# A GLA and short-convolution decoder step on one core: the sample's states through column groups of the array, and another order around the last head's norm

## The chip, the core and the metric

The kernel runs on one NeuronCore of a Trainium2 chip. Its engines work side by side and wait for each other through semaphores: TensorE (PE, matrix products; its weight loads are listed as PEld), VectorE (DVE), ScalarE (ACT), GpSimd (POOL), and SyncE (SP), which here only issues DMAs. The metric is the device time of one execution in microseconds, the median of several runs. The profile is one further execution taken by the hardware profiler; its span is the time from its first to its last instruction.

## What is computed

One inference step of a two-layer decoder, width 1024. The tokens are one new sequence of 1024 tokens (the prompt) and 8 running sequences with 4 new tokens each (the sample). Layer 0 mixes with gated linear attention (GLA, 4 heads, key width 128, value width 256), layer 1 with a gated short convolution; each is followed by an MLP of width 4096, and each of the four parts ends with a LayerNorm of the scaled residual:

```python
x = layer_norm(ALPHA * x + h, ln1_g[i], ln1_b[i])                       # h: the mixer
x = layer_norm(ALPHA * x + mlp(x, mlp_w_up[i], mlp_w_down[i]), ln2_g[i], ln2_b[i])
```

In the GLA, a head's output is a part within the chunk of tokens and a part from the recurrent state, `o_inter = q_dec S_prev`, with a state of 128 x 256. The prompt starts from a zero state. Each of the 8 sample sequences brings its own state per head, so its four query columns meet a matrix that no other sequence uses. Everything is f32, and all outputs include the new states.

## The kernel before

Activations are kept transposed, channels on the 128 partitions and tokens along the free axis: Z holds 8 chunks of channels by 1056 tokens. In the GLA stage the tokens are worked on in three groups (`TGS`): 384, 384 and 288 columns, the last with 256 prompt tokens and the 32 of the sample. Big products split each f32 operand into a high and a low part in fp32r and run three passes (`mm3`, L234); small ones use plain f32 products (`mm`, L230), of which the profile lists two records each.

**A head.** `queries_keys` projects the queries and keys of the three groups, `core` (L588) walks the nine token tiles (eight of the prompt, the ninth the sample), `gated` (L572) projects the output gate of a group, applies SiLU (ScalarE) and multiplies (VectorE), then splits into `hh` and `hl`; `accumulate` (through `out(tg)`) multiplies by the output weights and adds into Z. For the ninth tile `core` calls `sample` (L667): `outputs` forms the 32 output columns from the values and the masked scores (`sTs`) and from the states: for each of the 8 sequences and each half of the value width one product of 128x128 state weights with 4 query columns. `products` and `state` then update the states through four row groups of the array, 32 rows each. In the profile, `raw` in these products is the buffer that holds the states.

**Delayed steps.** Work that belongs beside other work is put into chains by `after(key, (delay, step), ...)`. A counter, `clock`, advances by an estimate of PE's time with each product (`cost`); `tick()`, called after each projection or block of products, runs each chain's next step if its delay has passed; `need(key)` runs all that is left of a chain at once. This sets the order in which instructions are written. In this part of the kernel each engine's final order is set by the tile framework, which may place later work earlier where an engine would stand idle; in the MLP part the DMA queues of SP and POOL keep the written order.

**The last head and its LayerNorm.** The mean is already taken out: the output weights are centred, and Z is centred during the heads. `accumulate` squares each chunk (ScalarE), adds the squares (VectorE and POOL), and `layer_norm` (L315) runs four steps: `split` (sum and split of the squares), `var` (two products with ones), `rstd` (L289 to L297: logarithm, exponential and a Newton step), and `finish` for each of four pairs of chunks (one multiplication of two chunks on VectorE, L334, then scale and bias of each chunk on ScalarE, L336). The order in the last head is `gated` for all three groups, then `out(0)`, `out(1)`, `out(2)`, then `need` for the three norms.

**The MLP.** Products use a Strassen-like scheme with seven products over quarters; the first two, 1 and 2, read only the first 528 token columns, product 5 the others too. A product of the up-projection has 8 steps of 24 matmuls of 2 x 264 columns. Before it, its four blocks of activations are split into `bh` (ScalarE, L847) and `bl` (VectorE, L848), in a ring of five buffers; the weights likewise into `wh` and `wl`. A `big` buffer holds the differences for product 5.

Of the kernel before, what the change touches and what calls it, by code (L numbers as in the profile page):

```python
# [57 lines left out]
def hybrid_step(ctx, tc, x_prompt, x_sample, state_gla, state_conv, gla_w_in, gla_w_gate_up, gla_b_gate,  # L58
# [33 lines left out]
    ident = const.tile([P, P], F32, name="ident")  # L92
    make_identity(nc, ident)
# [56 lines left out]
    for g in (2, 3):  # L150
        V.tensor_add(seq, seq, seq1[:, g, :])

# [163 lines left out]
    def layer_norm(tg, sums, pg, pb):  # L316
# [3 lines left out]
        box = {}  # L320

# [10 lines left out]
        def finish(k):  # L332
            pair = z[:, k:k + 2, :]
            V.tensor_tensor(pair, pair, box["rstd"][:, :n].unsqueeze(1).to_broadcast([P, 2, n]), op=ALU.mult)  # L334
# [126 lines left out]
    with tc.tile_pool(name="gp", bufs=3) as gp:  # L461
# [110 lines left out]
        def gated(tg, m, ur, o, tags=("g", "g")):  # L572
# [9 lines left out]
            hh = gt(tags[0], [P, 384], 9 if tags[0] == "g" else 3, F32R)  # L582
            A.copy(hh[:, :n], sr[:, :n])
            hl = gt(tags[1], [P, 384], 9 if tags[1] == "g" else 3, F32R)
# [3 lines left out]
        def core(h, qkk, uv, dec, o):  # L588
# [77 lines left out]
            def sample(k2t, st, vt):  # L666
# [33 lines left out]
                after(("sample",), (0, outputs))  # L700
# [31 lines left out]
        for h in range(H):  # L732
# [34 lines left out]
            for tg in range(3):  # L767
                tags = [("g", "g")] * 2
# [22 lines left out]
    for tg in range(3):  # L791
# [21 lines left out]
    cbuf = work.tile([P, KC * 34], F32, name="cbuf")  # L813
# [54 lines left out]
    class Unit:  # L868
# [33 lines left out]
        def split(self):  # L902
# [3 lines left out]
            return self.parts  # L906

# [20 lines left out]
    def up(x, pairs, relu):  # L928
# [62 lines left out]
        for prod in UP:  # L991
            for i, (s, quad) in enumerate(pairs):
# [386 lines left out]

    mlp(0, Z, Z2)  # L1380
# [55 lines left out]
```

## Time and profile before

| | us |
|---|---|
| median of 3 runs | 2261.52 |
| lowest and highest run | 2258.97, 2264.5 |
| profiled execution, its own time | 2263.59 |
| span of the profiled execution | 2261.9 |
| mean granted TensorE clock, share of full | 0.983 |
| busy: PE, DVE, ACT, POOL | 2202.5, 1619.5, 1127.8, 524.7 |
| GLA stage, from the start to PE's last GLA product | about 513 |

A line of the profile names the line of the kernel, the engine, the operation, the tiles it writes and reads, and shapes. The page counts a matmul as busy until its modelled end, so consecutive ones overlap; the distance from start to start is what a product costs in a stream. Idle time before an instruction stands in brackets with what ended it. `ps` and `pq` are accumulators in PSUM, `g`, `ring` and `raw` buffers in SBUF.

### The profile page before, as it was taken

Reading aid. Unit: us, or ns where it says so; the run is one execution under the profiler, and the core shown is the slowest. Engines: PE = TensorE matmul, PEld = TensorE weight load, DVE = VectorE, ACT = ScalarE, POOL = GpSimd, SP = SyncE. Lnnn points to the kernel's source line nnn. Section 1 sums busy time; section 2 is a strip of 40 time slices with the busy share of each in tenths; the row PEclk is TensorE's granted clock in tenths of the full one; section 3 lists DMA queues with packets and bytes.
Section 4 is the critical chain, followed back from the end, with each engine's and each line's share of the span. In section 5 each row is a group of like instructions: output and inputs, shape, how many; then the busy total and the mean of one; then the engine's idle time right before and its main releaser. Section 6 shows DMA issues by size and latency. Waiting matters only on the chain. (4 is left out here: it accounts for less than half of the span.)

```text
span 2261.9 us, 43193 instructions
## 1 busy us (share of the span) xinstructions
PE 2202.5 (97%) x17341; PEld 2180.1 (96%) x17341; DVE 1619.5 (72%) x2982; ACT 1127.8 (50%) x2023; POOL 524.7 (23%) x551
## 2 busy tenths in 40 slices
PE   9999999996999999999999999998999999999996
PEld 8999999996999999999999999997999999999996
DVE  7474848467578864678787897996668875578877
ACT  4443525258563445564457444445855444654443
POOL 5202321221422021412021323220331101422121
PEclk9999999998999999999999999998999999999998
DMA  5120212113868456769353857760786734877546
GB/s 156 32 75 31 75 40 67 38 59 81 109 119 214 119 108 122 97 126 217 99 112 68 131 111 100 164 156 24 126 136 141 177 90 95 129 131 185 152 88 148
DMA packets 297476, 251.51 MB, mean 111 GB/s; under 512 B 15444, under 2 KB 238776, under 8 KB 297276
## 3 DMA queue, kind: packets, MB, share of 16 engines
q0 software_dynamic: 123200, 107.58, 31.2%
q1 hardware_dynamic: 174076, 141.18, 21.1%
q8 instruction: 136, 2.23, 0.4%
q14 instruction: 64, 0.52, 0.1%
HBM read 227.00 MB, written 9.12 MB: 104 GB/s over the span
## 5 line engine op out<-in xcount | busy, mean ns | idle before, releaser
L865 PE MATMUL pq<-bh,wh 128*128 128x264 f32 x4160 | 847.6, 285 | 9.3 <-ACT bh L847 7.3
L865 PE MATMUL pq<-bl,wh 128*128 128x264 f32 x4160 | 847.7, 285 | 5.0 <-DVE bl L848 5.0
L865 PE MATMUL pq<-bh,wl 128*128 128x264 f32 x4160 | 845.0, 285 | 1.8 <-DVE wl L848 1.7
L865 PEld LDWEIGHTS pq<-bh,wh 128*128 128x128 f32 x4160 | 646.2, 189 | 11.5 <-ACT bh L847 9.9
L865 PEld LDWEIGHTS pq<-bl,wh 128*128 128x128 f32 x4160 | 646.3, 189 | 6.1 <-DVE bl L848 5.8
L865 PEld LDWEIGHTS pq<-bh,wl 128*128 128x128 f32 x4160 | 646.2, 189 | 2.6 <-DVE wl L848 2.5
L847 ACT CAST wh<-raw 128x512 fp32r<-128x512 f32 x312 | 193.5, 621 | 398.2 <-PE pq L865 383.7
L848 DVE TENSOR_TENSOR wl<-raw,wh 128x512 fp32r<-128x512 f32 x312 | 214.4, 688 | 142.2 <-ACT wh L847 135.2
L854 POOL DMA_DIRECT2D SB<-in_mlp_w_up x128 | 163.5, 1329 | 430.8 <-DVE wl L848 223.8
L847 ACT CAST wh<-SB 128x512 fp32r<-128x512 f32 x208 | 128.7, 619 | 239.2 <-PE pq L865 213.4
L848 DVE TENSOR_TENSOR wl<-SB,wh 128x512 fp32r<-128x512 f32 x208 | 142.7, 686 | 85.3 <-ACT wh L847 85.3
L847 ACT CAST bh<-H 128x528 fp32r<-128x528 f32 (+1 forms) x292 | 165.3, 570 | 56.7 <-PE pq L865 51.3
L848 DVE TENSOR_TENSOR bl<-H,bh 128x528 fp32r<-128x528 f32 (+1 forms) x292 | 179.0, 625 | 15.4 <-ACT bh L847 15.2
L854 POOL DMA_DIRECT2D SB<-in_mlp_w_down x96 | 85.1, 1172 | 300.3 <-DVE wl L848 136.6
L236 PE MATMUL ps<-XH,whi 128*128 128x384 f32 (+1 forms) x384 | 128.6, 335 | 0.0
L237 PE MATMUL ps<-XL,whi 128*128 128x384 f32 (+1 forms) x384 | 127.5, 332 | 0.0
L238 PE MATMUL ps<-XH,wlo 128*128 128x384 f32 (+1 forms) x384 | 127.0, 331 | 0.0
L854 POOL DMA_DIRECT2D SB<-in_conv_w_in x48 | 61.2, 1295 | 168.8 <-DVE wl L848 60.4
L865 PE MATMUL pq<-bh,rh 128*128 128x264 f32 x320 | 94.0, 294 | 4.0 <-ACT bh L847 4.0
L865 PE MATMUL pq<-bl,rh 128*128 128x264 f32 x320 | 91.9, 287 | 0.2
L865 PE MATMUL pq<-bh,rl 128*128 128x264 f32 x320 | 91.5, 286 | 0.0
L963 ACT ACTIVATE H<-H 128x528 f32<-128x528 f32 x96 | 61.9, 645 | 46.9 <-DVE H L983 28.0
(275 smaller groups left out, 3620.4 us busy)
## 6 DMA issues: line engine op xcount, KB each, us to landing
raw<-in_mlp_w_down SPq DMA_DIRECT2D x160, 256.0 KB, 3.2
SB<-in_mlp_w_up POOLq DMA_DIRECT2D x128, 256.0 KB, 4.9
raw<-in_mlp_w_up SPq DMA_DIRECT2D x96, 256.0 KB, 2.9
SB<-in_mlp_w_down POOLq DMA_DIRECT2D x96, 256.0 KB, 7.8
SB<-in_mlp_w_up SPq DMA_DIRECT2D x64, 256.0 KB, 4.3
raw<-in_gla_w_in SPq DMA_DIRECT2D x24, 512.0 KB, 3.8
SB<-in_conv_w_in POOLq DMA_DIRECT2D x48, 256.0 KB, 4.8
raw<-SB POOLq DMA_DIRECT2D x36, 256.0 KB, 4.2
```

The costliest lines, as they stand in the source:

```text
L236: PE.matmul(out, wh, xh, start=first, stop=False)
L237: PE.matmul(out, wh, xl, start=False, stop=False)
L238: PE.matmul(out, wl, xh, start=False, stop=last)
L847: A.copy(hi[:, :w], src)
L848: V.tensor_sub(lo[:, :w], src, f32(hi[:, :w]))
L854: queue.dma_start(dst, src, **kw)
L865: PE.matmul(out[:, c:c + NT], w, b[:, n * NT:(n + 1) * NT], start=first and i == 0, stop=last and i == 2)
L963: A.activation(h, h, AF.Relu, scale=sign)
```

## The change

Four things are done.

- `sample`: a new step, `inter`, multiplies the 32 query columns (as 128x32 weights) with the states. For each half of the sequences four products of 256 columns go to four 32-partition strips of one PSUM bank, that is, to four column groups of the array. Each strip then holds all 32 query columns against one sequence's state; two VectorE operations pick the valid rows with the mask `seq` and add the halves into `x`. `outputs`, at least 2000 ns of PE's estimated time later, adds `x` to the output through one product per half of the value width with `rep4`, a matrix that folds the four strips back into 32 columns. The sixteen 4-column products go.
- The last head runs `out(0)` and `out(1)` before `gated` of the third group; the buffers' tags that the old order called for go.
- In `layer_norm`, the third group only stores the summed squares in `cbuf`, which is made at the start; the rest becomes `last_tokens`, a chain in the MLP with a delay of 3000 before each step. Its result is needed at product 5.
- In `layer_norm`, the second group's delays shrink, and every second chunk's scale and bias moves to VectorE.

```diff
+    rep4 = gconst.tile([P, NS], F32, name="rep4")
+    V.tensor_add(rep4, ident[:, 0:NS], ident[:, NS:2 * NS])
+    for g in (2, 3):
+        V.tensor_add(rep4, rep4, ident[:, g * NS:(g + 1) * NS])
...
+        if tg == 2:
+            V.tensor_add(cbuf, sums[0][:, :n], sums[1][:, :n])
+            return
...
-                A.activation(z[:, i, :], z[:, i, :], AF.Identity, scale=par[:, pg + i:pg + i + 1],
-                             bias=par[:, pb + i:pb + i + 1])
-        after(("x", tg), (1500, split), (D_VAR - 1500, var), (D_RSTD, rstd), *[(D_FIN, lambda k=k: finish(k)) for k in range(0, KC, 2)])
+                g, b = par[:, pg + i:pg + i + 1], par[:, pb + i:pb + i + 1]
+                if i == k:
+                    A.activation(z[:, i, :], z[:, i, :], AF.Identity, scale=g, bias=b)
+                else:
+                    V.tensor_scalar(z[:, i, :], z[:, i, :], g, b, op0=ALU.mult, op1=ALU.add)
+        d_var, d_rstd, d_fin = (1500, 100, 100) if tg else (D_VAR - 1500, D_RSTD, D_FIN)
+        after(("x", tg), (1500, split), (d_var, var), (d_rstd, rstd), *[(d_fin, lambda k=k: finish(k)) for k in range(0, KC, 2)])
...
+                def inter():
+                    pi = ps()
+                    for j in range(2):
+                        for g in range(4):
+                            PE.matmul(pi[g * NS:(g + 1) * NS, j * DV:(j + 1) * DV], q_[:, off:off + NS], s0[j][:, g, :],
+                                      start=True, stop=True)
+                    cost(DV, 8)
+                    x = ring()[:, :DV]
+                    V.tensor_scalar(x, pi[:, 0:DV], seq[:, 0:1], None, op0=ALU.mult)
+                    V.scalar_tensor_tensor(x, pi[:, DV:2 * DV], seq[:, 1:2], x, op0=ALU.mult, op1=ALU.add)
+                    box.append(x)
                 def outputs():
+                    x = box.pop()
...
                         mm(po[:, m * NS:(m + 1) * NS], vt[:, ms], st, stop=False)
-                        for i in range(NSEQ):
-                            c = i * LSEQ
-                            mm(po[:, m * NS + c:m * NS + c + LSEQ], s0[i // 4][:, i % 4, ms],
-                               q_[:, off + c:off + c + LSEQ], start=False, stop=i == NSEQ - 1)
+                        mm(po[:, m * NS:(m + 1) * NS], x[:, ms], rep4, start=False)
...
-                after(("sample",), (0, outputs))
+                after(("sample",), (0, inter), (2000, outputs))
...
                 if last and tg == 2:
-                    tags = [("b", "g"), ("b", "b")]
-                hs.append([gated(tg, m, ur[m], o[tg], tags[m]) for m in range(2)])
+                    out(0)
+                    out(1)
+                hs.append([gated(tg, m, ur[m], o[tg]) for m in range(2)])
...
             if last:
-                explog()
-                out(0)
-                out(1)
-            if last:
                 out(2)
...
     explog()
-    for tg in range(3):
+    for tg in range(2):
         need(("x", tg))
...
+    def last_tokens():
+        n, z = TGS[2][1], ACC[2]
+        room = big()
+        v, y, t = (room.rearrange("p a b -> p (a b)")[:, i * n:(i + 1) * n] for i in range(3))
+        box = {}
...
+        after(("x", 2), (3000, split_), (3000, var), (3000, rstd_),
+              *[(3000, lambda k=k: finish(k)) for k in range(0, KC, 2)])
...
                         if prod == 5:
                             need(("ln", 1))
+                            need(("x", 2))
...
+    last_tokens()
     mlp(0, Z, Z2)
```

In `last_tokens`, `split_` splits `cbuf` into a buffer pair of the `b` ring, `var` is two products into a PSUM buffer of the MLP, `rstd_` the same operations as before with their intermediates in the `big` buffer, and `finish` the same four pairs, with all scales and biases on ScalarE.

More of the change, by code (lines that the diff above doesn't have):

```diff
@@ L92, in hybrid_step @@
     ident = const.tile([P, P], F32, name="ident")
+    cbuf = const.tile([P, 288], F32, name="cbuf")
     make_identity(nc, ident)
@@ L570, in rms, with gated @@
             after(("rms", tg), (300, squares), (1500, split), (1500, var), (500, norm))
-        def gated(tg, m, ur, o, tags=("g", "g")):
+        def gated(tg, m, ur, o):
             n = TGS[tg][1]
@@ L581, in gated @@
             V.tensor_mul(sr[:, :n], o[:, m, :n], sr[:, :n])
-            hh = gt(tags[0], [P, 384], 9 if tags[0] == "g" else 3, F32R)
+            hh = gt("g", [P, 384], 9, F32R)
             A.copy(hh[:, :n], sr[:, :n])
-            hl = gt(tags[1], [P, 384], 9 if tags[1] == "g" else 3, F32R)
+            hl = gt("g", [P, 384], 9, F32R)
             V.tensor_sub(hl[:, :n], sr[:, :n], f32(hh[:, :n]))
@@ L812, in hybrid_step @@
     SB = work.tile([P, NB, 512], F32, name="SB")
-    cbuf = work.tile([P, KC * 34], F32, name="cbuf")
     cst = cbuf[:, 0:KC * 16].rearrange("p (j s) -> p j s", s=16)
```

21 lines of the change are left out of this document (20 added, 1 removed).

## The prediction

> **What bounds the kernel now.** I read the busy table of the page first, then TensorE's own timeline around the places where it is not streaming at full rate, then the granted clock over short windows.
>
> ```profile
> PE 2202.5 (97%) x17341; PEld 2180.1 (96%) x17341; DVE 1619.5 (72%) x2982; ACT 1127.8 (50%) x2023; POOL 524.7 (23%) x551
> ```
>
> TensorE (PE) is busy 97% of the span, so time can come only from three things: matmuls that disappear, its few idle stretches, or a higher clock. The longest idle stretch is the handover from the attention mixer to the first MLP. These are PE's four consecutive entries there (start us, duration, line, operation; the idle time before each in brackets):
>
> ```profile
> 522.76 0.61 PE L309 MATMUL ps<-ring,ones_r 128*128 128x288 f32 x1 [9.52 <-DVE ring L304]
> 523.60 0.61 PE L310 MATMUL ps<-ring,ones_r 128*128 128x288 f32 x1 [0.23 <-DVE ring L305]
> 531.13 1.69 PE L865 MATMUL pq<-bh,wh 128*128 128x264 f32 x6 [6.93 <-ACT bh L847]
> 533.96 0.81 PE L865 MATMUL pq<-bl,wh 128*128 128x264 f32 x2 [1.14 <-DVE bl L848]
> ```
>
> Idle: 9.52 + 0.23 + 6.93 + 1.14 = 17.8 us, broken only by the third token group's variance product. The dense stream then starts at half clock. The row for 531.13 to 538.90 (busy PE, PEld, DVE, ACT, POOL; granted clock; DMA) shows 0.50:
>
> ```profile
> 531.13:538.90 7.77, 6.63 (x28) 6.32 (x29) 7.77 (x14) 7.77 (x14) 0.00 (x0) 0.50 0.16 46
> ```
>
> Who holds PE there is the vector engine (DVE): from the end of `out(1)` (506.35) to the first `bl` block (533.20) it is busy 25.13 of 26.85 us.
>
> ```profile
> 506.35:533.20 26.85, 9.79 (x60) 8.51 (x58) 25.13 (x44) 20.14 (x40) 7.21 (x7) 0.72 0.10 30
> ```
>
> The second place is the sample part of each head. PE's timeline in the last head:
>
> ```profile
> 461.42 0.30 PE L232 MATMUL ps<-sTs,vt 128*128 128x32 f32 x2
> 461.55 1.93 PE L232 MATMUL ps<-g,raw 128*128 128x4 f32 x16
> 463.34 0.39 PE L232 MATMUL ps<-sTs,vt 128*128 128x32 f32 x2
> 463.56 3.34 PE L232 MATMUL ps<-g,raw 128*128 128x4 f32 x16
> 466.76 0.67 PE L236 MATMUL ps<-XH,whi 128*128 128x384 f32 x1
> ```
>
> PE has work here throughout, but its products stream four columns against a full 128x128 weight load. In each of the four heads the clock goes to half during or right after it (same columns, PE only):
>
> ```profile
> 102.00:105.40 3.40, 3.40 (x14) 0.50 0.00 0
> 221.50:228.30 6.80, 6.80 (x25) 0.50 0.23 60
> 344.40:347.80 3.40, 3.40 (x13) 0.51 0.00 1
> 463.90:470.70 6.80, 6.80 (x27) 0.50 0.00 0
> ```
>
> That is 20.4 us at half speed: 10.2 us lost, on an engine that is busy and on the critical path all the while.
>
> **Part 1: the sample's states.** Removed per head: two passes of one 32-column and eight 4-column products. The first pass ran at full clock from 461.42 to 463.34, 1.92 us, so both cost 3.84 us undisturbed. Added: eight products with 32 weight columns and 256 streamed columns (`inter`), two DVE operations, and in `outputs` two 32-column products with `rep4` beside the two with `sTs` that stay.
>
> The trace has no column-grouped product. Its nearest row is the state update, which sends eight products of 256 f32 columns through the four row groups of the array:
>
> ```profile
> 472.64 0.34 PE L238 MATMUL ps<-XH,wlo 128*128 128x384 f32 x1
> 472.90 1.15 PE L232 MATMUL ps<-vt,ring 32*128 32x256 f32 x16
> 473.98 0.45 PE L236 MATMUL ps<-XH,whi 128*128 128x384 f32 x1
> ```
>
> The product at 472.64 takes its usual 0.17 us, so the eight occupy 472.81 to 473.98, 1.17 us with the change of tiling at both ends. If groups did not overlap, the price would be that of plain f32 products, 128 columns in 0.22 us:
>
> ```profile
> 451.54 0.39 PE L232 MATMUL ps<-sT,vt 128*128 128x128 f32 x2
> 451.76 0.39 PE L232 MATMUL ps<-qx,S 128*128 128x128 f32 x2
> ...
> 452.96 0.28 PE L237 MATMUL ps<-wlo,XH 128*32 128x256 f32 x1
> ```
>
> Eight of 256 columns are then 8 x 0.44 = 3.5 us. I take 1.17, the end next to the only row with grouped products, and keep 3.5 for the range; nothing suggests a price below 1.17. The Trainium skill ("TensorE: Matmul & The Clock Gate", Part 3) gives a factor of 2.38 for three column groups; if four did no better, the estimate from that page would be 3.5 / 2.38 = 1.5 us, and my final time 1.2 us later. No run here shows it yet.
>
> The four 32-column products cost 0.13 us (461.42 to 461.55) to 0.22 us (463.34 to 463.56) each, say 0.7 us together. So a head pays 1.17 + 0.7 = 1.9 instead of 3.84 us: 4 x 1.95 = 7.8 us. The half-clock stretches should go too: the row-grouped products at 472.90 are followed by none, and the quarter-array products at 452.96, 24 in a row, run at full clock:
>
> ```profile
> 452.00:456.50 4.50, 4.50 (x41) 1.00 0.01 4
> ```
>
> Together **7.8 + 10.2 = 18.0 us**. The added wait is that of `outputs` on `x`: behind it in PE's queue stands the next projection. `inter` is issued one projection earlier (24 products of 384 columns at 0.17 us, 4.2 us), and `x` needs two DVE operations of 256 columns, about 0.9 us by the 0.45 of a 288-column one (529.06, below). DVE has room in the last head, but little soon after the sample of head 2 (354 to 364):
>
> ```profile
> 354.00:359.00 5.00, 5.00 (x31) 5.00 (x30) 5.00 (x11) 4.10 (x5) 2.40 (x3) 1.00 0.00 0
> 359.00:364.00 5.00, 3.69 (x22) 3.45 (x21) 5.00 (x8) 1.01 (x2) 4.67 (x6) 1.00 0.43 139
> 461.00:466.00 5.00, 5.00 (x37) 5.00 (x35) 1.27 (x3) 2.81 (x4) 0.00 (x0) 0.78 0.02 8
> ```
>
> There DVE is full and PE already loses 1.3 of 5 us. With 0.9 us more on DVE, the state products one projection later, and PE arriving sooner, I charge **1 us** (0 to 3). `rep4` is three 32-column additions at the start, nothing.
>
> **Part 2: the handover.** Three edits, one answer: `gated(2)` now runs after `out(1)`, the second group's norm no longer waits for ticks, and the third group's norm goes into the first products. PE gets two projections of 24 products more to do behind `out(1)`; a 288-column product takes (510.74 - 510.35) / 3 = 0.13 us:
>
> ```profile
> 510.35 0.29 PE L236 MATMUL ps<-b,whi 128*128 128x288 f32 x1
> 510.48 0.30 PE L237 MATMUL ps<-g,whi 128*128 128x288 f32 x1
> 510.61 0.29 PE L238 MATMUL ps<-b,wlo 128*128 128x288 f32 x1
> 510.74 0.29 PE L236 MATMUL ps<-b,whi 128*128 128x288 f32 x1
> ```
>
> That is 48 x 0.13 = 6.3 us of cover. But DVE is the bound, so I count its queue from the end of `out(1)` to the first `bl`. It took 26.85 us. The prices (start to start in DVE's timeline):
>
> ```profile
> 529.06 0.45 DVE L296 SCALAR_TENSOR_TENSOR ring<-ring,ring 128x288 f32<-128x288 f32 x1
> 529.43 0.68 DVE L848 TENSOR_TENSOR wl<-raw,wh 128x512 fp32r<-128x512 f32 x1
> 530.03 0.45 DVE L297 SCALAR_TENSOR_TENSOR ring<-ring,ring 128x288 f32<-128x288 f32 x1
> 530.52 2.77 DVE L334 TENSOR_TENSOR Z<-Z,ring 128x576 f32<-128x576 f32 x4
> 533.20 1.32 DVE L848 TENSOR_TENSOR bl<-Z,bh 128x528 fp32r<-128x528 f32 x2
> ```
>
> An operation over 288 columns is 0.37 us, a weight split 0.60, the third group's four pairs 2.7. Two more rows, grouped by shape (busy us, mean ns):
>
> ```profile
> L296 DVE SCALAR_TENSOR_TENSOR ring<-ring,ring 128x384 f32<-128x384 f32 x2 | 1.7, 855 | 0.0
> L297 DVE SCALAR_TENSOR_TENSOR ring<-ring,ring 128x384 f32<-128x384 f32 x2 | 1.1, 549 | 0.0
> ```
>
> and, from the same view of the whole execution:
>
> ```profile
> L1210 DVE TENSOR_SCALAR Z<-Z,par 128x528 f32<-128x528 f32 x32 | 15.6, 559 | 2.4 <-ACT Z L1206 2.3
> ```
>
> Leaves this queue: the third group's norm, seven operations (7 x 0.37 = 2.6) and four pairs (2.7), and two weight splits that come behind the first `bl` (1.2): 6.5 us. Joins it: the addition into `cbuf` (0.4), the four operations of `gated(2)` (1.5), and the eight affine steps that move from ScalarE to DVE, 0.40 us each (559 ns x 384 / 528): 3.2; in all 5.1 us. The first `bl` comes 26.85 - 6.5 + 5.1 = 25.45 us after `out(1)` instead of 26.85: 1.4 us earlier, and `out(1)` itself ends 6.3 us earlier for having `gated(2)` behind it. That is 7.7 us, the lower bound, if the queue keeps its own 1.7 us of gaps and the operations slowed beside POOL's additions (L296 took 855 ns on average over 384 columns, its sister L297 549; such operations add up to some 1.5 us, an estimate). Without these it is 10.9. I take the middle, **9.3 us**. PE's own path has room for this: it waits some 3 us for the last operands of `gated(2)` (a SiLU, a product and a split behind the last projection, with DVE full), then ends `out(2)` at about 6.3 + 0.3 + 3 + 6.3 = 16 us, well ahead of 25.45. That new wait costs nothing while DVE is the bound; if DVE were not, it would cost its 3 us. The restart at half clock stays, as the idle stretch is still some 8 us.
>
> The third group's norm then runs beside the first two products. The stretch of these two had room on DVE, less on ScalarE (ACT):
>
> ```profile
> 541.20:579.50 38.30, 38.30 (x317) 38.30 (x317) 16.39 (x26) 32.08 (x53) 11.64 (x9) 1.00 0.81 158
> ```
>
> PE pays 0.3 us for the variance products, once in its idle time. Three things can be late: the norm takes one of five `b` buffers, so all four blocks of product 2 wait for product 1's last reads; `big` is held by the norm until its last pair, so product 5's differences, made early before, start some two steps before use; ACT's norm steps share 38 us with 32 busy. I charge **1 us** for these (0 to 3).
>
> **Sum:** 18.0 - 1.0 + 9.3 - 0.3 - 1.0 = 25.0 us. The profiled execution took 2263.59 us (span 2261.9, 1.7 around it): 2238.6. It lies 2.1 us above the median of the three runs, 2261.52, against which the result is measured: **2236.5 us**.
>
> **Rivals.**
>
> A, *the handover becomes smooth*: the first `bl` goes ahead of the later pairs of the norm, since product 1 needs only four of the eight chunks. Then PE is the bound: it loses 3 us in front of `out(2)`, about 1 for the first blocks and 2 at half clock. Before, it lost 17.8 idle and half of 538.9 - 533.96, 2.5, in all 20.3; so 14 instead of 9.3, some 2232 us, and 2229 if the waits overlap too. For it: at 531.13 PE ran six `bh` products before any `bl`, so an engine's order is not the program's everywhere. Against it: DVE ran all four pairs from 530.52 before `bl` at 533.20, in the order of the program.
>
> B, *the column groups don't overlap*, the change doesn't do what it says: 4 x (3.5 - 1.17) = 9.3 us less gain: 2246 us. For it: only row groups are seen overlapping, and in the groups of columns four different streams have to enter the array. Against it: eight row-grouped products had to share the same array and did it in a third of the serial time.
>
> C, *the clock still drops in each head*: the sample's new products follow a burst with a quarter of the array and are short. All of 10.2 us stays lost: 2247 us. Against it: the clock of 1.00 at 452 to 456.5. The Trainium skill ("TensorE: Matmul & The Clock Gate", Part 1) says that the gate answers to the array's activity in windows of about 3.4 us; the trace agrees, with dips of one and two such lengths, and shows them with PE busy throughout.
>
> D, *product 5 starves*: the third group's norm isn't done in the shadow of products 1 and 2. From its variance product (522.76) to its last pair (530.52 + 2.77) it took 10.5 us in the old handover; if PE came to wait for all of that, with a half-clock stretch behind it (1.7 to 3.4 us), 13 us: 2250 us. It decides only if ACT or DVE fall more than ten of the sixteen steps behind; with DVE busy 16 of 38 us I see no reason.
>
> E, *slower*: PE stands at `outputs` waiting for `x` in each head. If DVE is more than about 8 us behind, PE idles 4 us and more, and such a pause brings its own half-clock stretch (1.7 to 3.4 us lost, by the dips above). At a wait of 5 us: 4 x (5 + 2.6) = 30 us, 2267 us. Below 3.6 us per head the kernel is still faster. The row 461 to 466, DVE busy 1.27 of 5, speaks against it.
>
> **How the numbers follow.** Forecast 0.58, A 0.13, B 0.12, C 0.06, D 0.06, E 0.03, no effect 0.02. The forecast's own bounds: 18.0 + 10.9 - 0.3 = 28.6 with no charges (2233), 18.0 + 7.7 - 0.3 - 6 = 19.4 with both at 3 us (2242). To hold 8 in 10 the range takes in A with both charges at nothing (2228, with some margin for the spread of the runs, 2226) and B and C: 2226 to 2248. A measurement of this kernel can tell about 0.2%, 4.5 us, from no change: below 2257.0 counts as faster: forecast, A, B, C and D, 0.93 after a little for mixtures of the bad cases; same 0.04; slower 0.03.
>
> **What would show it.** Part 1: the eight products at `inter` within about 1.2 us, and no row of 0.50 after the samples (else B, C). `outputs` without idle time in front (else E). Handover: PE's first MLP matmul still waits for `bh` and `bl`, some 8 us behind the end of `out(2)`, and DVE is full over that stretch; a gap under 4 us is A. Product 5's first matmul without a wait over 1 us (else D). The prediction is wrong above all if the column groups run one after another, or if DVE's order at the handover is not the program's.

## The result

| | before | after |
|---|---|---|
| median, lowest and highest run (us) | 2260.55 (2258.97 to 2264.5), 4 runs | 2237.88 (2236.81 to 2239.01), 4 runs |
| ratio of the medians | | 0.9897, 95% interval 0.988 to 0.9914 |
| profiled execution (us), its span | 2263.59, 2261.9 | 2239.01, 2237.3 |
| mean granted TensorE clock | 0.983 | 0.990 |

The kernel became 22.7 us faster by the medians and 24.6 us by the profiled executions. The forecast was 2236.5 us, in a range of 2226 to 2248.

### The profile after

The busy table of the page, after: TensorE (PE) is busy for 19.0 us less (2202.5 before; part of that is half clock that is gone) and is still the bound.

```profile
PE 2183.5 (98%) x17293; PEld 2157.5 (96%) x17293; DVE 1625.9 (73%) x3000; ACT 1116.6 (50%) x2013; POOL 524.9 (23%) x551
```

**The sample.** PE's timeline in the last head, after (start us, duration, line, operation). The eight column-grouped products are the row of L693:

```profile
450.09 1.07 PE L693 MATMUL ps<-raw,g 128*32 128x256 f32 x16
451.10 0.45 PE L243 MATMUL ps<-XH,whi 128*128 128x384 f32 x1
...
455.37 0.30 PE L239 MATMUL ps<-sTs,vt 128*128 128x32 f32 x2
455.51 0.39 PE L239 MATMUL ps<-rep,ring 128*128 128x32 f32 x2
...
456.18 0.42 PE L243 MATMUL ps<-XH,whi 128*128 128x384 f32 x1
```

The eight products take 1.01 us from start to start (451.10 - 450.09). One projection later the four 32-column products take 456.18 - 455.37 = 0.81 us, with no idle time in front of them: `x` is there.

The granted clock around the four samples, after (columns: window, its length, PE busy, clock, DMA share, GB/s). The windows lie where the kernel before ran at half clock, shifted to the new times:

```profile
95.00:110.00 15.00, 15.00 (x109) 1.00 0.25 74
215.00:230.00 15.00, 15.00 (x104) 1.00 0.13 35
335.00:350.00 15.00, 14.25 (x94) 1.00 0.13 37
450.00:465.00 15.00, 15.00 (x108) 1.00 0.00 1
```

Where the kernel before had lost 1.31 us of PE behind the sample of head 2, PE's timeline after shows

```profile
350.99 0.41 PE L316 MATMUL ps<-ring,ones_r 128*128 128x288 f32 x1 [1.74 <-DVE raw L723]
...
358.46 0.40 PE L243 MATMUL ps<-XH,whi 128*128 128x288 f32 x1 [0.39 <-ACT ring L299]
```

2.1 us, so 0.8 us more.

**The handover.** PE's timeline after, at the entries that correspond to the four shown of before:

```profile
491.18 1.20 PE L243 MATMUL ps<-g,whi 128*128 128x288 f32 x7 [0.39 <-ACT g L599]
...
505.04 1.69 PE L887 MATMUL pq<-bh,wh 128*128 128x264 f32 x6 [7.18 <-ACT bh L869]
509.51 0.81 PE L887 MATMUL pq<-bl,wh 128*128 128x264 f32 x2 [2.79 <-DVE bl L870]
```

PE idles 7.18 + 2.79 = 10.0 us where it idled 17.8. Two short waits ahead of these are new: the 0.39 us shown, and 0.44 us at 482.56. The vector engine (DVE) is busy 24.27 of the 24.87 us from the end of `out(1)` (483.88) to the first `bl`; its timeline up to there, after:

```profile
501.06 2.66 DVE L345 TENSOR_TENSOR Z<-Z,ring 128x768 f32<-128x768 f32 x2
503.64 1.33 DVE L351 TENSOR_SCALAR Z<-Z,par 128x384 f32<-128x384 f32 x2
...
507.79 0.68 DVE L870 TENSOR_TENSOR wl<-raw,wh 128x512 fp32r<-128x512 f32 x1
508.39 0.45 DVE L330 TENSOR_TENSOR cbuf<-ring,ring 128x288 f32<-128x288 f32 x1
508.75 2.56 DVE L870 TENSOR_TENSOR bl<-Z,bh 128x528 fp32r<-128x528 f32 x4
```

**A measure that is free of what lies elsewhere.** The span also holds what changes from one execution to the next in other stages. So I take two instants in each trace: the last head's eighth tile (PE's last product with `ident` there, ahead of that head's sample) and DVE's addition that ends the eighth and last step of product 2 of the first MLP. In the trace of after they are

```profile
441.05 0.27 PE L625 MATMUL ps<-ident,ring 128*128 128x128 f32 x1
```

and

```profile
559.77 0.70 DVE L1026 TENSOR_TENSOR H<-H,pq 128x528 f32<-128x528 f32 x1
```

and of before

```profile
452.43 0.27 PE L609 MATMUL ps<-ident,ring 128*128 128x128 f32 x1
```

and

```profile
583.49 0.70 DVE L970 TENSOR_TENSOR H<-H,pq 128x528 f32<-128x528 f32 x1
```

The first instant moved by 11.4 us (heads 0 to 2), the second by 23.7 us. The distance between them, which holds the last head's sample and the handover, fell from 131.06 to 118.72 us, by 12.34. What comes later in the profiled pair adds 24.6 - 23.7 = 0.9 us, which I put down to no edit. The two parts of the 12.34 us are told apart below.

### The profile page after: what moved, and what is told of

Its sections match the earlier page's. It is cut to its first block, busy times and chain, and to the rows that moved or that the text cites. A ratio compares the mean times of both kernels' runs of the same rounds, so it can differ in the third digit from the quotient of the medians.

```text
span 2237.3 us, 43108 instructions
## 1 busy us (share of the span) xinstructions
PE 2183.5 (98%) x17293; PEld 2157.5 (96%) x17293; DVE 1625.9 (73%) x3000; ACT 1116.6 (50%) x2013; POOL 524.9 (23%) x551
## 5 line engine op out<-in xcount | busy, mean ns | idle before, releaser
L870 DVE TENSOR_TENSOR bl<-H,bh 128x528 fp32r<-128x528 f32 (+1 forms) x292 | 179.3, 626 | 14.6 <-ACT bh L869 14.3
L243 PE MATMUL ps<-whi,XH 128*128 128x256 f32 (+1 forms) x288 | 84.5, 293 | 0.0
```

The lines of the kernel that those rows point to most:

```text
L243: PE.matmul(out, wh, xh, start=first, stop=False)
L870: V.tensor_sub(lo[:, :w], src, f32(hi[:, :w]))
```

## The experiments

Theory at the start: the gain has two independent parts, the sample (fewer PE us and no half clock) and the handover, where DVE's queue ahead of the first `bl` sets the time, so that each operation taken from that queue counts. Rivals: the sample gains by the clock alone; the handover gains by PE's order alone. The last column is the distance between the two instants in the profiled execution; how long the handover's half clock lasts differs by up to 3.4 us from one execution to the next, so up to 1.7 us of the distance are uncertain (shown in the last section).

| run | what | median (range), us | ratio to before, 95% interval | distance, us |
|---|---|---|---|---|
| `e1_sample_only` | before + sample | 2245.14 (2243.85 to 2247.57) | 0.9934 (0.9921 to 0.9946) | 125.33 |
| `e2_handover_only` | after, old sample | 2251.72 (2248.76 to 2253.9) | 0.9956 (0.9943 to 0.997) | 124.94, against 131.06 |
| `e3_one_strip` | after, one column group | 2246.98 (2245.35 to 2247.98) | 0.9939 (0.9926 to 0.9951) | not taken |
| `e4_two_halves` | before, old products in two parts | 2255.05 (2253.43 to 2256.97) | 0.9978 (0.9968 to 0.9987) | not taken |
| `e5_affine_act` | after, all scale and bias on ScalarE | 2237.67 (2237.1 to 2240.11) | 0.9898 (0.9883 to 0.9913) | 118.72 |
| `e6_late_act` | e5, half of them behind product 1's first blocks | 2237.97 (2237.18 to 2241.91) | 0.99 (0.9886 to 0.9915) | 119.01 |
| `e7_norm3_in_place` | after, third norm at the handover | 2238.23 (2237.59 to 2238.84) | 0.9897 (0.9881 to 0.9914) | 119.14 |
| `e8_old_order` | after, old order of the last head | 2241.01 (2239.81 to 2241.24) | 0.9907 (0.989 to 0.9923) | 120.85 |
| `e9_old_delays` | after, old delays | 2238.75 (2236.96 to 2239.44) | 0.9899 (0.9884 to 0.9914) | 118.89 |
| `e10_warm` | after + 130 matmuls in the idle time | 2240.12 (2238.6 to 2240.62) | 0.9903 (0.9888 to 0.9918) | 119.97 |
| `e11_order_alone` | e1 + new order only | 2239.75 (2238.57 to 2240.55) | 0.9902 (0.9888 to 0.9917) | 119.98 |
| `e12_warm95` | after + 95 matmuls | 2236.81 (2235.8 to 2238.87) | 0.9895 (0.9879 to 0.9912) | 117.13 |

### The two parts alone: `e1_sample_only`, `e2_handover_only`

The first is the kernel before with `inter`, `rep4` and the new `outputs`, nothing else; the second the changed kernel with the old sample (its edit against the changed kernel):

```diff
-                def inter():
...
                 def outputs():
-                    x = box.pop()
                     po = ps()
...
-                        mm(po[:, m * NS:(m + 1) * NS], x[:, ms], rep4, start=False)
+                        for i in range(NSEQ):
+                            c = i * LSEQ
+                            mm(po[:, m * NS + c:m * NS + c + LSEQ], s0[i // 4][:, i % 4, ms],
+                               q_[:, off + c:off + c + LSEQ], start=False, stop=i == NSEQ - 1)
...
-                after(("sample",), (0, inter), (2000, outputs))
+                after(("sample",), (0, outputs))
```

> The kernel before with only the sample's part (inter, rep4, the new outputs). By the traces of before and after, the four heads gained 3.5, 5.15, 2.4 and 5.2 us, 16 in all: 14 to 18 us faster than before, no stretch at half clock in the heads. Rival, the handover carries most of the gain and the heads' freed time is waited for again at the handover: less than 10 us.

> The changed kernel with the sample's part as before: the new order in the last head, the second group's delays, the third group's norm in the MLP. Theory: 8 us faster than before (6 to 10), half-clock stretches in the heads as before, first bl block about 25 us behind the end of out(1). Rival: both parts need each other, under 4 us.

Measured: 15.1 us less than before (2260.28 in that comparison) for the sample, 8.6 us for the handover. Their sum, 23.7, is within 1 us of the 22.7 that both bring together, so no dependence of the parts shows, and both expectations held. In the trace of the first, the handover stands as before (PE's timeline):

```profile
504.89 0.61 PE L314 MATMUL ps<-ring,ones_r 128*128 128x288 f32 x1 [9.52 <-DVE ring L309]
505.73 0.61 PE L315 MATMUL ps<-ring,ones_r 128*128 128x288 f32 x1 [0.23 <-DVE ring L310]
513.26 1.69 PE L881 MATMUL pq<-bh,wh 128*128 128x264 f32 x6 [6.93 <-ACT bh L863]
516.08 0.81 PE L881 MATMUL pq<-bl,wh 128*128 128x264 f32 x2 [1.13 <-DVE bl L864]
```

Its distance is 125.33 us. So of the 12.34 us, 5.73 are the last head's sample and 6.61 the handover; the sample has 11.4 + 5.7 = 17.1 us in the profiled pair. `e2_handover_only` gives 131.06 - 124.94 = 6.12 us for the handover.

### Do four column groups run at once? `e3_one_strip`

All eight products go to the same 32 partitions, so to one column group. Three quarters of the sample's states are left out of the output, and the two VectorE operations work on these 32 partitions, with the rest of `x` set to zero.

```diff
-                            PE.matmul(pi[g * NS:(g + 1) * NS, j * DV:(j + 1) * DV], q_[:, off:off + NS], s0[j][:, g, :],
+                            PE.matmul(pi[0:NS, j * DV:(j + 1) * DV], q_[:, off:off + NS], s0[j][:, g, :],
...
```

> The changed kernel, but all eight products of inter go to the same strip of 32 partitions, so to one column group (it leaves out the contributions of three quarters of the sample's states; one memset and the same two DVE operations over 32 partitions remain). If the gain of inter rests on four groups running at once, the eight products take about 3.5 us instead of 1.1 and the kernel is 4 x 2.4 = 9.6 us slower than the changed one, some 2247 us, with the clock still at full rate after the samples. If successive products overlap anyway, no change. If a quarter of the array counts as too little activity, the half-clock stretches come back: another 7 to 10 us.

Measured: 9.1 us more than the changed kernel, and in PE's timeline

```profile
453.90 3.64 PE L693 MATMUL ps<-raw,g 128*32 128x256 f32 x16
```

3.64 us in one group against 1.07 in four: the four groups overlap by a factor of 3.4. Four heads x 2.57 us = 10.3 us, of which the median shows 9.1. The Trainium skill ("TensorE: Matmul & The Clock Gate", Part 3) gives 2.38 for three column groups; the estimate from that page for these eight would be 3.64 / 2.38 = 1.53 us. The measurement decides: 1.07. The clock stayed at 1.00 here too, behind the samples of all four heads: it is not the short duration of the grouped products that spares it.

### The clock by itself: `e4_two_halves`

The kernel before, with the same sixteen 4-column products of each head; those of the second value half only come one projection later (`half(m)` writes the products of one value half). Nothing is removed.

```diff
-                after(("sample",), (0, outputs))
+                after(("sample",), (0, lambda: half(0)), (2000, outputs))
```

> The kernel before with the same 4-column products, but the first value half's sixteen records one projection earlier than the second's, so each burst is 1.9 us instead of 3.8 with 4 us of dense products between. If the clock falls because a window of 3.4 us sees mostly 4-column products, the four half-clock stretches go away: 8 to 10 us faster than before with no instruction removed. If any such burst trips the gate, the stretches stay and the time is that of before within 2 us.

Measured: 5.2 us less than before. The two parts in the first head, by PE's timeline,

```profile
95.37 1.93 PE L232 MATMUL ps<-g,raw 128*128 128x4 f32 x16
...
101.58 1.93 PE L232 MATMUL ps<-g,raw 128*128 128x4 f32 x16
```

and the granted clock from 80 to 500 us

```profile
80.00:500.00 420.00, 416.79 (x2934) 1.00 0.18 55
```

where the same window of before has 0.98:

```profile
80.00:500.00 420.00, 418.69 (x2893) 0.98 0.18 55
```

So the half clock comes with some 3.8 us of 4-column products in one run; two runs of 1.93 us with dense work between them don't bring it. Not every long run does, either: behind that of the first head in the trace of `e2_handover_only` the clock stays at 1.00. What decides it is worked out in the last section.

The size is less clear. The profiled pair agrees with the expectation of 8 to 10 us (2263.59 - 2253.71 = 9.9 us), the medians don't (5.2): the profiled execution of before lies 3.3 us above the median of this comparison, that of `e4_two_halves` 1.3 us below its own. Two causes can be seen, and neither was measured by itself. The half clock differs between executions: the trace of before has six windows of 3.4 us of it in the heads, 10.2 us lost, and that of `e2_handover_only`, with the same products, five (8.5 us lost, none in the first head). And `e4_two_halves` gives some time back: from 80 to 490 us PE idles 3.21 us, where before has 1.31. So the sample's gain can't be divided sharply between clock and products: for the products 15.1 - 5.2 = 9.9 us by medians, 17.1 - 10.2 = 6.9 by the profiled pair, where 7.8 were counted.

### Is each operation in DVE's queue on the path? `e5_affine_act`, `e6_late_act`, `e7_norm3_in_place`, `e9_old_delays`

`e5_affine_act` gives the eight scales and biases back to ScalarE (DVE has eight operations less before `bl`); `e6_late_act` also writes those of chunks 4 to 7 behind product 1's first blocks; `e7_norm3_in_place` puts the third group's norm back to the handover; `e9_old_delays` restores the delays.

`e5_affine_act`:

```diff
-                if i == k:
-                    A.activation(z[:, i, :], z[:, i, :], AF.Identity, scale=g, bias=b)
-                else:
-                    V.tensor_scalar(z[:, i, :], z[:, i, :], g, b, op0=ALU.mult, op1=ALU.add)
+                A.activation(z[:, i, :], z[:, i, :], AF.Identity, scale=g, bias=b)
```

> The changed kernel with all scale-and-bias steps of the first two groups' norm on ScalarE again. If the vector engine's queue sets when the first bl block comes, eight operations of 0.39 us leave it: the block comes 1 to 2.5 us earlier (ScalarE, with two steps per pair and then the bh blocks, is next), 1 to 2.5 us faster than the changed kernel (2237.9). Rival, ScalarE is the bound there and the move to the vector engine is what pays: 1 to 3 us slower.

`e6_late_act`:

```diff
-                g, b = par[:, pg + i:pg + i + 1], par[:, pb + i:pb + i + 1]
-                if i == k:
-                    A.activation(z[:, i, :], z[:, i, :], AF.Identity, scale=g, bias=b)
+                if k < KC // 2:
+                    affine(i, True)
                 else:
-                    V.tensor_scalar(z[:, i, :], z[:, i, :], g, b, op0=ALU.mult, op1=ALU.add)
+                    late.append(lambda i=i: affine(i, True))
...
                         box["b"] = blocks(prod, box)
+                        while late:
+                            late.pop(0)()
```

> The changed kernel with all scale-and-bias steps of the first two groups on ScalarE, and those of chunks 4 to 7, which product 1 doesn't read, written behind the first blocks of product 1. If the queue theory holds, neither engine has them in front of the first block any more: first bl about 3 us earlier, 2.5 to 3.5 us faster than the changed kernel. If only the pairs' multiplications and the logarithm chain count, no more than 1 us.

`e7_norm3_in_place`:

```diff
-        if tg == 2:
-            V.tensor_add(cbuf, sums[0][:, :n], sums[1][:, :n])
-            return
...
-    for tg in range(2):
+    for tg in range(3):
         need(("x", tg))
...
-    last_tokens()
```

> The changed kernel with the third group's norm at the handover as before, all else as changed. Queue theory: seven operations of 0.37 us and four pairs of 0.67 us come in front of the first bl, less the addition into cbuf: 4.9 us, so 4 to 6 us slower than the changed kernel, 2242 to 2244. Rival, PE's own last products set the handover: under 1.5 us.

`e9_old_delays`:

```diff
-        d_var, d_rstd, d_fin = (1500, 100, 100) if tg else (D_VAR - 1500, D_RSTD, D_FIN)
+        d_var, d_rstd, d_fin = D_VAR - 1500, D_RSTD, D_FIN
```

> The changed kernel with the second group's delays as before (6000, 500, 1000). Its variance products come one block of out(2) later, but the vector engine took up the result only 6 us after them in the changed kernel's trace (490.45, then 496.32), so the queue doesn't notice: within 0.7 us of the changed kernel. Rival, the chain itself is the bound: 2 us slower or more.

Measured: none of the four moved the median by more than 0.9 us from 2237.88, and the ranges of all overlap with that of the changed kernel. Three of the four expectations missed: `e5_affine_act` (1 to 2.5 us faster) and `e6_late_act` (2.5 to 3.5 us faster) gained nothing, and the norm in place, for which 4 to 6 us more had been expected, cost nothing clear of the scatter. DVE's timeline of `e7_norm3_in_place` shows why there:

```profile
505.37 0.44 DVE L330 TENSOR_TENSOR ring<-ring,ring 128x288 f32<-128x288 f32 x1
505.73 0.69 DVE L866 TENSOR_TENSOR bl<-Z,bh 128x528 fp32r<-128x528 f32 x1
506.35 0.29 DVE L311 CAST ring<-ring 128x288 fp32r<-128x288 f32 x1
506.57 0.69 DVE L866 TENSOR_TENSOR bl<-Z,bh 128x528 fp32r<-128x528 f32 x1
507.19 0.44 DVE L312 TENSOR_TENSOR ring<-ring,ring 128x288 fp32r<-128x288 f32 x1
507.56 0.69 DVE L866 TENSOR_TENSOR bl<-Z,bh 128x528 fp32r<-128x528 f32 x1
...
512.37 1.43 DVE L341 TENSOR_TENSOR Z<-Z,ring 128x576 f32<-128x576 f32 x2
```

The norm is written ahead of the blocks, but on the engine its operations and the blocks alternate, and its pairs (L341) come behind all four `bl`. (Before the change, the pairs stood ahead of `bl`.) So the first `bl` comes at the same place as in the changed kernel: 505.73 - 438.03 = 67.7 us behind the first instant, and 508.75 - 441.05 = 67.7 there. What PE waits for instead is the norm itself, whose two variance products stand ahead of the MLP's in PE's order (PE's timeline of `e7_norm3_in_place`):

```profile
506.70 0.61 PE L316 MATMUL ps<-ring,ones_r 128*128 128x288 f32 x1 [11.86 <-DVE ring L311]
507.69 0.61 PE L317 MATMUL ps<-ring,ones_r 128*128 128x288 f32 x1 [0.38 <-DVE ring L312]
```

PE's first product with a low part thereby came 2.0 us later than in the changed kernel (508.54 - 438.03 = 70.5 us behind the first instant, against 509.51 - 441.05 = 68.5), but its half-clock stretch then lasted 2.1 us (to 510.6) instead of 4.6 (to 514.1), so about 1.2 us came back. By the medians the deferral brings 0.35 us, by the distance 0.4, and with half clocks of equal length it would be about 1.7 (an estimate: the 2.0 us less the 0.3 of the variance products, which the changed kernel has later).

Without the scales and biases on DVE, ScalarE is what PE waits for instead (PE's timeline of `e5_affine_act`; here `bl` no longer ends any wait):

```profile
505.83 1.03 PE L884 MATMUL pq<-bh,wh 128*128 128x264 f32 x3 [10.30 <-ACT bh L866]
506.66 0.72 PE L884 MATMUL pq<-bl,wh 128*128 128x264 f32 x2
```

The first product with a low part comes at 506.66 - 437.90 = 68.8 us behind the first instant of its trace, where the changed kernel has 68.5: the work only changed its queue. In `e6_late_act` DVE is free of the eight operations, and four of ScalarE's, those of the second group, come behind the first blocks (the first group's run early all the same). The first `bl` still comes 24.66 us behind the end of `out(1)`, against 24.87 in the changed kernel. DVE is busy for only 22.08 us of that: it now waits 1.00 us for ScalarE's `g`, 0.67 for PE's `ps` and 0.31 for ScalarE's `ring`. So a full DVE did not mean that each of its operations delays `bl`. My theory of the queue had fallen; what was left was the order.

### The order: `e8_old_order`, `e11_order_alone`

The first takes only the new order out of the changed kernel, the second puts only the new order into `e1_sample_only`. The edit of the second (the first is its reverse; the tags of the buffers go with it):

```diff
             for tg in range(3):
-                tags = [("g", "g")] * 2
                 if last and tg == 2:
-                    tags = [("b", "g"), ("b", "b")]
-                hs.append([gated(tg, m, ur[m], o[tg], tags[m]) for m in range(2)])
+                    out(0)
+                    out(1)
+                hs.append([gated(tg, m, ur[m], o[tg]) for m in range(2)])
...
-            if last:
-                explog()
-                out(0)
-                out(1)
             if last:
                 out(2)
```

> The changed kernel with one thing put back: the last head multiplies its third token group's gate values first and its three output products after them, as before. Everything else of the change stays (sample, deferred third norm, split scale and bias, shorter delays). Order theory (the 8 us of the handover are all from having out(0) and out(1) ahead of the gate products of the third group, so that these cover the second norm): 5 to 8 us slower than the changed kernel, 2243 to 2246 us. Rival (the gain is spread over the four edits of the handover, each covering for the others, as the three runs without loss may be read): under 2 us slower, at most 2240 us.

> The kernel before with the new sample and the new order of the last head, and nothing else of the change: the third norm in place at the handover, all scale and bias on ScalarE, the old delays. Order theory: within 1.5 us of the changed kernel, 2237 to 2239.5 us. Rival (the deferred norm, the split of scale and bias and the delays bring something only together): at least 3 us slower than the changed kernel, 2241 to 2245 us; 2245 is what the new sample alone gave.

Measured: without the order 3.1 us slower than the changed kernel (the ranges don't touch), which neither expectation had. With the order alone it is 1.9 us slower, between the two expectations; there the ranges overlap, so that it can't be told from the 1.5 us of the first. It is 5.4 us faster than `e1_sample_only`. By the distances, the order alone brings 125.33 - 119.98 = 5.35 of the 6.61 us, the other three edits alone 125.33 - 120.85 = 4.48; by medians 5.4 and 4.1 of 7.3. They overlap: each hides most of the same wait. PE's waits with the old order,

```profile
492.74 0.69 PE L316 MATMUL ps<-ring,ones_r 128*128 128x384 f32 x1 [1.94 <-DVE ring L311]
...
506.64 1.69 PE L890 MATMUL pq<-bh,wh 128*128 128x264 f32 x6 [8.58 <-ACT bh L872]
510.37 0.81 PE L890 MATMUL pq<-bl,wh 128*128 128x264 f32 x2 [2.04 <-DVE bl L873]
```

and with the order alone

```profile
489.20 0.53 PE L241 MATMUL ps<-g,whi 128*128 128x288 f32 x2 [1.34 <-ACT g L588]
...
505.73 0.61 PE L314 MATMUL ps<-ring,ones_r 128*128 128x288 f32 x1 [9.52 <-DVE ring L309]
506.70 0.61 PE L315 MATMUL ps<-ring,ones_r 128*128 128x288 f32 x1 [0.36 <-DVE ring L310]
508.47 0.81 PE L877 MATMUL pq<-bl,wh 128*128 128x264 f32 x2 [0.65 <-DVE bl L860]
```

say the same: 10.6 and 10.5 us idle at the handover itself, against 17.8 before and 10.0 in the changed kernel. The first line of each is a wait ahead of it. With the old order the second group's variance product stands among the products of `out(2)` and holds PE for 1.94 us, and a half clock of 3.4 us follows it (492.7 to 496.2, 1.7 us lost). In the kernel before, the same product (512.72) waits for nothing. So part of what `e8_old_order` loses comes from the old order together with the other edits, probably with the shorter delays; this pair was not run by itself, and which of the three others hides the wait was not separated either.

### The idle time that is left: `e10_warm`, `e12_warm95`

The changed kernel restarts at half clock (window, length, PE busy, clock, DMA share, GB/s):

```profile
504.00:509.00 5.00, 1.69 (x6) 0.50 0.01 2
509.00:514.00 5.00, 4.49 (x20) 0.50 0.34 98
514.00:519.00 5.00, 5.00 (x43) 0.98 0.40 115
```

From 509.51 to about 514.1 dense products run at half speed: 2.3 us lost. Extra matmuls, whose result nobody reads, fill the idle time (95 in the second kernel):

```diff
+    warm = ps2()
+    for i in range(130):
+        PE.matmul(warm[:, 0:P], ones_r, ones_r, start=True, stop=True)
     last_tokens()
```

> The changed kernel with 130 matmuls of ones by ones (128 columns, result never read) on TensorE between the last output product and the first product of the next stage, where it stood idle for 7 us and then ran at half clock to about 514 us. Theory (the half clock is the price of the idle time and costs about half of the dense stretch from 509.5 to 514.2, 2.4 us): clock 1.00 from the first product on and 1.5 to 2.5 us faster than the changed kernel, 2235.5 to 2236.5 us. Rival (the second gap, in which the first products wait for the low parts of their operands, drops the clock again, or the extra matmuls hold up the first products): no change or up to 2 us slower.

> As the run with 130 extra matmuls, but with 95. There one took 0.1125 us, so the 130 ended 2.7 us after the first low part was there and the first product waited for them; 95 would end at 506.6 in that trace, 1 us before the first low part is written. Theory (the half clock after the idle time is a price that can be avoided): clock 1.00 throughout and the first product 3 us earlier than with 130, so 1.5 to 2 us faster than the changed kernel: 2235.5 to 2237 us. Rival (the gap of about 1 us that is left drops the clock again, or what follows eats the gain): 2238 us or more.

130 were too many: they ran until the blocks had long been ready, and the kernel was 2.2 us slower. With 95, PE's timeline is

```profile
495.26 10.72 PE L1439 MATMUL pq<-ones_r 128*128 128x128 f32 x95
...
507.10 0.51 PE L887 MATMUL pq<-bl,wh 128*128 128x264 f32 x2 [0.83 <-DVE bl L870]
```

and the clock over the restart

```profile
504.00:509.00 5.00, 4.17 (x35) 1.00 0.18 52
509.00:514.00 5.00, 5.00 (x44) 1.00 0.55 156
```

The first product with a low part comes at the same place as in the changed kernel (507.10 - 438.61 = 68.5 us behind the first instant), now at full clock, and the distance is 1.6 us shorter. So the half clock is a price of the idle time and can be avoided. The median is 1.07 us lower, within what was expected, but the ranges overlap: over the whole kernel the gain can't be told from nothing. It is the lowest median of all runs.

## Why the prediction held, and where it was off

- **The sample, 18.0 less 1.0.** Right, step by step, in the profiled pair. The eight products were put at 1.17 us and took 1.01 (start to start), the four 32-column ones at 0.7 and took 0.81. No half clock is left after the samples. The part brought 17.1 us in the profiled pair and 15.1 by medians. The charge of 1 us for head 2, where DVE is full, was about right: 0.8 us. Rivals B (the groups run one after another) and C (the clock still drops) are out: 3.64 against 1.07 us, and 1.00 in all windows. E didn't occur, as no product of `outputs` waits.
- **The handover, 9.3 less 0.3 and 1.0.** The size was off: 6.6 us by the distance, 7.3 by medians (2245.14 - 2237.88). The first `bl` came 508.75 - 441.05 = 67.7 us behind the first instant; in `e1_sample_only` it starts at 515.33, 75.4 us behind. That is 7.7 us earlier, the lower bound of the count, and the choice of the middle was the mistake. That it met the bound so closely is luck: `out(1)` ended 5.7 us earlier, where 6.3 were counted (48.5 and 42.8 us behind the first instant), and the stretch from there to `bl` became 2.0 us shorter, where 1.4 were counted. About 1.1 us of the 7.7 is not seen at the end of product 2: 0.3 are the third norm's variance products there, about 0.2 the longer half clock (4.6 us against 4.2 in `e1_sample_only`), and the rest is open.
- **Its mechanism was half right.** DVE is full up to `bl`, as forecast, and the first `bl` came 24.87 us behind the end of `out(1)` (483.88), where 25.45 were counted. But the step "leaves this queue, joins it", in which each operation ahead of `bl` counts by itself, failed: putting the norm's operations back, or taking the eight scales off, moved the time by no more than the runs scatter. The queue's order is not the program's: with the norm in place, the blocks come between its steps and ahead of its pairs. The prediction named this as what would make it wrong, but read the four pairs ahead of `bl` in the old trace as a sign of the opposite. The sum of 6.3 us for the order and 1.4 for the queue failed as a sum, too: alone, the order gives 5.35 us and the other edits 4.48, of 6.61 together.
- **The wait for the last operands of `gated(2)`.** Forecast 3 us, measured 0.39: PE took seven products with `hh` first, and wasn't held up by `hl`. As said, it set nothing.
- **Later charge of 1 us, rival D.** PE doesn't idle from 515 to 1000 us, so product 5 does not starve; of the charge nothing is seen beyond the 1.1 us above.
- **Rival A** (under 4 us of waiting) didn't come: 10.0 us idle, and the half clock behind it. Its first step, blocks ahead of a norm's pairs, is seen for the third norm in `e7_norm3_in_place`, but PE's wait didn't fall by it.
- **From the profile to the median.** The sum of 25.0 gave 2238.6 us for a profiled execution, and 2239.01 was measured. That this is so close is in part luck: 1.4 us too much was counted for the handover (8.0 with its charges, 6.6 by the distance), and 0.9 us came from later stages, where nothing was forecast. The median was forecast 1.4 us too low, because the same 25.0 was taken off a median that lay 2.1 us under the profiled execution. If part of those 2.1 us was half clock, it was counted as a gain from a time that hadn't contained it. The mean clocks speak for it (0.983 in the profiled execution, 0.984 as the median of the runs; 0.001 of 2260 us is about 2 us, an estimate), and so do the six and five windows found in the two traces of the old sample; it is not shown for the median run itself.

## What to carry to other kernels

An engine that is 97% busy can still lose time at half clock: look at the granted clock in short windows around runs of narrow products, and first try to split such a run with dense work between (5.2 us here, for nothing removed) before replacing it. Where several edits hide the same wait, their prices don't add: take one out and put one in alone, since either test by itself says too much or too little. And the size of an effect that differs between executions, like the half clock here, is not read from one profiled execution: hold it against the times and granted clocks of the other runs.

## What was not expected of the hardware

- Four column groups with f32 products of 256 columns run 3.4 times as fast as one (3.64 to 1.07 us for eight).
- The clock can drop with PE busy throughout, after some 3.8 us of 4-column products against full weights, but not after two runs of 1.93 us, nor after 3.64 us of 256-column products that use a quarter of the columns.
- A 128-column product of fp32r took 10.72 / 95 = 0.113 us at a granted clock of 1.00, nearly as much as the 0.13 us of one of 288 columns in the prediction's rows. I had planned the 130 for some 9 us; they took 14.6.
- The half clock behind the handover's idle time lasted 2.1 to 4.6 us of dense work (`e7_norm3_in_place` and the changed kernel). The traces show a reason: the clock changes only at points that lie multiples of 3.41 us apart. With the old order (`e8_old_order`) it falls at 492.7, rises at 496.2, falls at 503.0 and rises at 513.2: one, two and three times 3.41 us. In the kernel before it falls at 463.8, rises at 470.6, falls at 518.4 and rises at 538.9: two, fourteen and six times. So where the work begins between two such points decides how much of it runs at half clock, which makes a restart uncertain by up to 1.7 us. The Trainium skill ("TensorE: Matmul & The Clock Gate", Part 1) says that the window which the gate watches runs freely, so that the point of change depends on where in it the work begins; these traces agree with that.
- These points cut each trace into windows, and they tell the long runs of 4-column products apart. The first window that such products fill to 62% or more is followed by half clock: 98, 95, 78 and 64% in the four heads before, 92, 78 and 62% in the last three heads of `e2_handover_only`. At 59% (its first head) and at 57% or less (all of `e4_two_halves`) the clock stays. So the same run costs a head nothing, one window of half clock or two (1.7 or 3.4 us lost), by where it lies.
